# New estimates for three groups of operations in a kernel whose order is planned from estimates

## The chip, the cores and the metric

The kernel runs on one core of a Trainium2 chip. The core has a matrix engine (PE in the profile, with its weight loads as PEld), a vector engine (DVE), a scalar engine (ACT), a general engine (POOL) and a queue that issues the transfers from HBM (SP). Each engine takes its own instructions in the order in which they stand in the program and waits at each for the semaphores of others. The metric is the device time of one launch in microseconds (us), as a median of several runs.

## The reference

Two blocks are computed one after the other on 256 tokens with 1024 features, in float32:

```python
def first_block(x, c, ...):                      # two layers
    mod = einsum('bd,ldm->lbm', silu(c), w_mod) + b_mod
    for i in range(2):
        sh_m, sc_m, g_m, sh_f, sc_f, g_f = split(mod[i], 6)
        h = x * (1 + sc_m) + sh_m
        y = even_mixer(h, ...) if i == 0 else odd_mixer(h, ...)
        x = layer_norm(ALPHA * x + (1 + g_m) * y, ...)
        h = x * (1 + sc_f) + sh_f
        x = layer_norm(ALPHA * x + (1 + g_f) * swiglu(h, ...), ...)
    return x

def hybrid_layer(h, ...):                        # second block, 16 + 256 tokens
    proj = rmsnorm(h) @ w_in                     # nine outputs of 1024
    o = hgrn2_chunked(q, k, v, log(f))           # recurrence over tokens
    merged = sigmoid(gate_a) * rmsnorm(o) * silu(g_out) + sigmoid(gate_b) * b * dwconv(c * x)
    h = h + merged @ w_out
    a, val = split(rmsnorm(h) @ w_up, 2)
    return rmsnorm(h + (silu(dwconv(a)) * val) @ w_down)
```

`even_mixer` holds two attentions (stick-breaking, and one over the 64 best keys of each query), `odd_mixer` the differential attention: two softmaxes per head, one taken from the other with a weight.

## The kernel before, in words

The matrices are read from HBM once, 230 MB in all, and split into two parts that the matrix engine takes in its one-pass float32 form: a slab lands in `stage`, ACT copies it rounded to `whi` (mm3's high part), DVE subtracts that copy from the slab to `wlo`, and every product is made three times (`mm3`: high by high, high by low, low by high). Most of PE's rows are such products with 256 or 258 columns. Six buffers each of `whi` and `wlo`, three of `stage` and three of `mst` bound how far the stream can run ahead.

`mst` is a second stream: the modulation matrix comes in 96 chunks of 512 KB, and DVE makes each into one column of `mod` (`mod_chunks`), one scalar_tensor_tensor per chunk. They are spread over the layers in which they are not yet needed.

Nothing in the program is written in its final order. All operations are recorded by `Plan` in the order of the mathematics, with a due time that is their number plus a bias (`LAG`, `XLAG`, `BIAS`). `Plan.order` (L246 on) then runs a list schedule: each engine takes, whenever it is free in the plan, the operation with the earliest due time of those whose inputs are ready and for which a buffer is free. How long an operation keeps its engine in the plan is what `Plan.cost` (L171 to L207) says. `Plan.issue` sends the operations out in that order, so that all instructions carry its line, L428 (L427 for ACT's table loads). What `cost` says is therefore never on the chip, but the order on each engine is what comes out of it, and so is the buffer that each tile gets.

The places of which the prediction speaks:

- `Norm.add` (L723 on) is called for the eight feature chunks of a residual. DVE makes the residual, ACT its square, DVE and ACT the operand of the next product, and POOL adds residuals and squares to two running sums, `lns1` and `lns2`. When the last chunk is in, PE sums both over the partitions by products with one column (`ps_s`, a constant by `lns1` or `lns2`), and all of the norm follows from these. Rows of the next product group (`norm.U`, 258 columns) can stand ahead of them on PE.
- `gen_diff` (L1225 on) is one head of the differential attention: a score product (`ps_i`) that needs `q` and `kz`, which DVE adds up from a half that POOL has multiplied (`rot`, in `rope_parts`); a softmax on DVE and ACT into `e`; a transpose of `e` on PE.
- `gen_hgrn` (L1446 on), called for two halves of the heads, starts with a chain of 14 small additions on POOL (`su`, L1456). ACT takes their exponential, DVE multiplies it into `kd`, and PE transposes `kd` (L1465).
- `Rms.add` (L1383 on) is the norm of the second block, with one running sum (`racc`) on POOL.

## Time and profile before

| | |
|---|---|
| median of 3 runs | 1172.05 us (1165.66 to 1173.66) |
| span of the profiled execution (first to last instruction) | 1163.9 us |
| PE busy | 1125.9 us, 97% of the span |
| DVE busy | 912.5 us, 78% |
| ACT busy | 726.0 us, 62% |
| POOL busy | 118.2 us, 10% |
| HBM read | 229.81 MB, 198 GB/s over the span |

The profile has one execution, and of that one the span is known and no time of its own beside it. A share of busy time is a mean over stages with different limits; what a change is worth is read from the stage, at the wait that ends last there. Times in the rows below are us from the start of the span, unless ns is said.

### The profile page before, as it was taken

To read this page: it belongs to the slowest core of one execution; us is meant where nothing else is said; L and a number is where in the kernel's file an instruction comes from. 1 tells how busy PE (TensorE), PEld (TensorE's weight loads), DVE (VectorE), ACT (ScalarE), POOL (GpSimd) and SP (SyncE) were. 2 spreads that over 40 slices of the span, in tenths; PEclk is the share of its full clock that TensorE was granted. 3 is DMA by queue.
4 is the path that set the end of the run, shared out by engine and by line. 5 is a ranking of instruction groups with operands and counts; after the bars stand their busy time and mean duration, and the time that the engine had idled before them with its cause. 6 is when DMAs were issued, how large, how long until landed. Compare 5 with 4: busy or idle time off the path is not lost.

```text
span 1163.9 us, 22101 instructions
## 1 busy us (share of the span) xinstructions
PE 1125.9 (97%) x8769; PEld 1077.6 (93%) x8769; DVE 912.5 (78%) x1676; ACT 726.0 (62%) x1316; POOL 118.2 (10%) x127
## 2 busy tenths in 40 slices
PE   5999989999999999999999999999999999999997
PEld 4885889999999779899999999999999999999996
DVE  6799889988999999885558896896659978866642
ACT  3558657545448987664445567786758766655541
POOL 0110220000231302200003402000010011000011
PEclk9999989999999999899999999999999999999999
DMA  9938647998985425365544625244433325555441
GB/s 352 410 131 309 236 163 279 350 328 301 339 327 193 143 104 194 140 246 189 181 171 178 232 88 182 86 169 154 172 110 145 144 100 193 200 188 189 168 163 37
DMA packets 42248, 232.29 MB, mean 200 GB/s; under 512 B 4640, under 2 KB 6176, under 8 KB 24096
## 3 DMA queue, kind: packets, MB, share of 16 engines
q1 hardware_dynamic: 42144, 230.87, 54.4%
q8 instruction: 69, 1.13, 0.4%
q14 instruction: 35, 0.29, 0.1%
HBM read 229.81 MB, written 1.05 MB: 198 GB/s over the span
## 4 chain that ended last, share of the span: by engine, by line
PE 77%; DVE 11%; ACT 4%; DMA 4%; issue 2%; POOL 2%; DVEq 0%; SPq 0%; ACTq 0%; POOLq 0%
PE pa L428 77%; DVE w L428 5%; DVE wlo L428 3%; ACT w L428 2%; DMA mst<-in_wmod_dram 2%; POOL w L428 2%; DVE sm L428 2%; DVE mst L428 1%; ACT whi L428 1%; DMA whi<-in_w_dram 1%; DMA cst<-in_cst_dram 1%; ACT L427 0%; DMA vec<-in_vecs_dram 0%; ACT sm L428 0%; ACT scb L428 0%
## 5 line engine op out<-in xcount | busy, mean ns | idle before, releaser
L428 PE MATMUL pa<-w,whi 128*128 128x256 f32 (+4 forms) x5104 | 919.4, 288 | 8.5 <-DMA whi<-in_w_dram 7.6
L428 PEld LDWEIGHTS pa<-w,whi 128*128 128x128 f32 x5104 | 769.7, 190 | 16.9 <-ACT w L428 6.3
L428 PE MATMUL pa<-w,wlo 128*128 128x256 f32 (+3 forms) x2608 | 661.5, 289 | 0.0
L428 ACT ACTIVATE whi<-stage 128x1024 fp32r<-128x1024 f32 (+1 forms) x330 | 339.5, 1041 | 247.7 <-PE pa L428 217.8
L428 DVE TENSOR_TENSOR wlo<-stage,whi 128x1024 fp32r<-128x1024 f32 (+1 forms) x330 | 404.1, 1234 | 100.3 <-ACT whi L428 94.0
L428 PEld LDWEIGHTS pa<-w,wlo 128*128 128x128 f32 x2608 | 465.5, 190 | 7.0 <-issue 3.9
L428 ACT ACTIVATE w<-w 128x256 fp32r<-128x256 f32 (+9 forms) x257 | 117.3, 470 | 80.6 <-DVE w L428 66.9
L428 POOL TENSOR_TENSOR w<-w,w 128x256 f32<-128x256 f32 (+2 forms) x93 | 84.1, 917 | 521.6 <-ACT w L428 291.2
L428 ACT ACTIVATE w<-pa 128x256 f32<-128x256 f32 (+12 forms) x298 | 108.0, 392 | 46.0 <-PE pa L428 41.7
L428 DVE TENSOR_TENSOR w<-w,w 128x256 fp32r<-128x256 f32 (+7 forms) x263 | 121.5, 480 | 19.2 <-ACT w L428 15.7
L428 DVE SCALAR_TENSOR_TENSOR mst<-mst,scb 128x1024 f32<-128x1024 f32 x90 | 109.3, 1226 | 11.8 <-DMA mst<-in_wmod_dram 11.8
L428 DVE TENSOR_TENSOR w<-w,pa 128x256 f32<-128x256 f32 (+2 forms) x146 | 58.9, 418 | 60.9 <-PE pa L428 51.1
L427 ACT ACT_TABLE_LOAD x63 | 80.8, 1283 | 1.8 <-PEq L1832 0.7
L428 PE MATMUL pa<-w,w 128*128 128x128 f32 (+8 forms) x340 | 71.6, 336 | 1.2 <-DVE w L428 0.9
L428 PEld LDWEIGHTS pa<-w,w 128*128 128x128 f32 (+4 forms) x340 | 42.8, 176 | 10.6 <-issue 2.8
L428 PE MATMUL pa<-cst,w 128*128 128x128 f32 (+4 forms) x218 | 38.8, 268 | 12.6 <-POOL w L428 6.3
L428 PEld LDWEIGHTS pa<-cst,w 128*128 128x128 f32 (+2 forms) x218 | 27.8, 167 | 22.1 <-issue 7.5
L428 POOL TENSOR_TENSOR w<-w 128x256 f32<-128x256 f32 x4 | 3.2, 801 | 392.3 <-DVE w L428 392.3
L428 PE MATMUL pa<-w 128*128 128x128 f32 x240 | 35.0, 275 | 0.2 <-DVE w L428 0.2
L428 PE MATMUL pa<-whi,w 128*128 128x512 f32 x96 | 32.9, 417 | 0.0
L428 PEld LDWEIGHTS pa<-w 128*128 128x128 f32 x240 | 31.4, 191 | 0.4 <-issue 0.4
L428 POOL TENSOR_TENSOR w<-w,sinT 128x512 f32<-128x512 f32 (+1 forms) x14 | 20.4, 1454 | 107.0 <-ACT w L428 82.3
(145 smaller groups left out, 541.3 us busy)
## 6 DMA issues: line engine op xcount, KB each, us to landing
mst<-in_wmod_dram SPq DMA_DIRECT2D x90, 512.0 KB, 5.5
stage<-in_wgu_dram SPq DMA_DIRECT2D x44, 1024.0 KB, 5.0
stage<-in_wi_dram SPq DMA_DIRECT2D x36, 1024.0 KB, 4.8
stage<-in_wup_dram SPq DMA_DIRECT2D x22, 1024.0 KB, 4.8
stage<-in_wd_dram SPq DMA_DIRECT2D x24, 896.0 KB, 4.5
stage<-in_w_dram SPq DMA_DIRECT2D x15, 1024.0 KB, 7.1
stage<-in_wo_dram SPq DMA_DIRECT2D x12, 1024.0 KB, 4.8
stage<-in_wd_dram SPq DMA_DIRECT2D x12, 1024.0 KB, 4.8
```

The lines of the kernel that those rows point to most:

```text
L427: self.nc.scalar.preload_act_table_set(tables[i])
L428: fn(*[real(a) for a in args], **{k: real(a) for k, a in kw.items()})
```

## The change

Only `Plan.cost` is changed. A product in the one-pass form of 256 columns or more is put at 0.452 ns per column rather than 1/2.4 (118.2 rather than 109.2 ns at 256). An operation of ACT or DVE that writes to fewer than 128 partitions gets 90 ns on top. POOL's operations, which had 100 ns and 2.2 ns per element, get formulas of their own: 60 and 0.87 for a memset, 200 and 1.0 for an affine_select, 260 and 2.45 for the rest (an addition of 256 columns: 887 rather than 663 ns, one of 8 columns: 280 rather than 118). No instruction is added or removed on PE, DVE, POOL or SP; the numbers set the order, the buffer of each tile and the places of ACT's table loads.

```diff
             if reads[0].dtype == F32:
                 return max(214.0, 4 * n / 2.4 + 5)
-            return (n if n >= 256 or reads[0].dtype == BF16 else 4 * n) / 2.4 + 2.5
+            if reads[0].dtype == BF16:
+                return n / 2.4 + 2.5
+            return 0.452 * n + 2.5 if n >= 256 else 4 * n / 2.4 + 5
         if eng == "ACT":
...
-            return src + n * 0.833 + 93.0 * ptr + (90.0 if len(writes) > 1 else 0.0)
+            held = 90.0 if writes[0].shape[0] < 128 else 0.0
+            return src + n * 0.833 + 93.0 * ptr + held + (90.0 if len(writes) > 1 else 0.0)
         if eng == "POOL":
-            return 100.0 + n * 2.2
+            if op == "memset":
+                return 60.0 + n * 0.87
+            if op == "affine_select":
+                return 200.0 + n * 1.0
+            return 260.0 + n * 2.45
...
-        return 66.0 + 64.0 * ptr + n * (0.52 if fast else 1.04)
+        held = 90.0 if writes[0].shape[0] < 128 else 0.0
+        return 66.0 + 64.0 * ptr + held + n * (0.52 if fast else 1.04)
```

What the order makes of it is shown at three places. In these rows the number behind a name is that of the tile's buffer and of the write that filled it; L428 of before is L436 of the change.

**The modulation stream.** SP's queue at the end of the first swiglu's down projection and the start of the second layer. Before:

```order
L428 DMA stage_3752<-in_w_dram 128x2048
L428 DMA mst_3789<-in_wmod_dram 128x1024
L428 DMA stage_3811<-in_w_dram 128x2048
L428 DMA mst_3850<-in_wmod_dram 128x1024
L428 DMA stage_3867<-in_w_dram 128x2048
L428 DMA mst_3907<-in_wmod_dram 128x1024
L428 DMA stage_3926<-in_w_dram 128x2048
L428 DMA mst_3969<-in_wmod_dram 128x1024
L428 DMA mst_3990<-in_wmod_dram 128x1024
```

And now, at the same place in the queue:

```order
L436 DMA mst_3512<-in_wmod_dram 128x1024
L436 DMA mst_3556<-in_wmod_dram 128x1024
L436 DMA stage_3566<-in_wd_dram 128x1792
L436 DMA stage_3612<-in_w_dram 128x2048
L436 DMA mst_3627<-in_wmod_dram 128x1024
L436 DMA mst_3640<-in_wmod_dram 128x1024
L436 DMA mst_3674<-in_wmod_dram 128x1024
L436 DMA stage_3694<-in_w_dram 128x2048
L436 DMA mst_3730<-in_wmod_dram 128x1024
```

Up to three chunks now stand between two slabs where there was one or two, and the slabs come later in the queue: ahead of the first slab of the second layer (`stage_3611` before, `stage_3612` now) there are 85 chunks of this stream rather than 77. DVE's own rows of the chunks move along. Before, the last ten of them ran between 349 and 512 us; now all stand ahead of the place that was reached at 349 us.

**The norm of the differential attention's residual.** PE, where the next product group (258 columns) meets the sums of the norm (`cst` by a running sum, 128x1). Before:

```order
L428 MATMUL pa_5488<-w_12_5254,whi_5418 128x258
L428 MATMUL pa_5486<-w_18_5259,whi_5402 128x258
L428 MATMUL pa_5488<-w_18_5259,whi_5418 128x258
L428 MATMUL pa_5486<-w_12_5254,wlo_5451 128x258
L428 MATMUL pa_5495<-w_12_5254,whi_5428 128x258
L428 MATMUL pa_5481<-w_12_5254,whi_5386 128x258
L428 MATMUL pa_5481<-w_18_5259,whi_5386 128x258
L428 MATMUL pa_5495<-w_18_5259,whi_5428 128x258
L428 MATMUL pa_5481<-w_12_5254,wlo_5415 128x258
L428 MATMUL pa_5486<-w_12_5254,whi_5402 128x258
L428 MATMUL pa_5508<-cst_100,w_4_5342 128x1
L428 MATMUL pa_5508<-cst_100,w_4_5431 128x1
```

Now:

```order
L436 MATMUL pa_5483<-w_12_5242,whi_5372 128x258
L436 MATMUL pa_5483<-w_18_5252,whi_5372 128x258
L436 MATMUL pa_5483<-w_12_5242,wlo_5397 128x258
L436 MATMUL pa_5491<-w_12_5242,whi_5400 128x258
L436 MATMUL pa_5493<-cst_100,w_3_5318 128x1
L436 MATMUL pa_5491<-w_18_5252,whi_5400 128x258
L436 MATMUL pa_5497<-w_12_5242,whi_5412 128x258
L436 MATMUL pa_5497<-w_18_5252,whi_5412 128x258
L436 MATMUL pa_5493<-cst_100,w_9_5367 128x1
L436 MATMUL pa_5493<-cst_100,w_3_5318 128x1
```

Fourteen rows of the next group stood ahead of the first sum; now it is four. On DVE, which feeds the sums, the third of four residuals moves behind two weight subtractions (`wlo`) and two operand splits that it stood ahead of.

**The small chain of the first HGRN half.** DVE, where it prepares POOL's chain: the product with 260 columns and the one after it belong to the convolution, the COPY of 4 columns is the chain's first value, and the pair 128x4x16 is `kd`, which waits for the chain. Before:

```order
L428 TENSOR_TENSOR w_7_8428<-w_7_8428,pa_8388 128x260
L428 TENSOR_SCALAR w_4_8443<-w_7_8428,vec_98 128x258
L428 COPY w_10_8450<-w_2_8279 128x4
L428 MEMSET w_10_8450 128x4 x2
L428 TENSOR_TENSOR wlo_8456<-stage_8156,whi_8433 128x1024
L428 TENSOR_TENSOR wlo_8476<-stage_8314,whi_8447 128x1024
L428 MEMSET w_10_8450 128x4
L428 SCALAR_TENSOR_TENSOR w_4_8443<-w_7_8428,vec_98,w_4_8443 128x258 x2
L428 MEMSET w_6_8515 128x256
L428 MEMSET w_3_8521 32x128
L428 TENSOR_TENSOR wlo_8525<-stage_8314,whi_8466 128x1024
L428 TENSOR_TENSOR w_6_8515<-w_10_8450,w_2_8279 128x4x16 x2
```

Now, the first rows and, behind three memsets and two rows of the convolution, the last:

```order
L436 TENSOR_TENSOR wlo_8387<-stage_8212,whi_8371 128x1024
L436 TENSOR_TENSOR wlo_8416<-stage_8289,whi_8400 128x1024
L436 TENSOR_TENSOR wlo_8429<-stage_8289,whi_8411 128x1024
L436 TENSOR_TENSOR wlo_8443<-stage_8326,whi_8424 128x1024
L436 TENSOR_TENSOR w_7_8436<-w_7_8436,pa_8396 128x260
L436 TENSOR_SCALAR w_10_8465<-w_7_8436,vec_98 128x258
L436 COPY w_3_8469<-w_2_8240 128x4
```

```order
L436 TENSOR_TENSOR wlo_8499<-stage_8326,whi_8448 128x1024
L436 TENSOR_TENSOR w_10_8465<-w_10_8465,pa_8450 128x258
L436 TENSOR_TENSOR wlo_8544<-stage_8404,whi_8528 128x1024
L436 TENSOR_TENSOR wlo_8561<-stage_8404,whi_8549 128x1024
L436 TENSOR_TENSOR w_6_8488<-w_3_8469,w_2_8240 128x4x16 x2
```

Four weight subtractions that stood behind the chain's first value now stand ahead of it, and between that value and `kd` there are again three, of later slabs. On ACT, in the same way, four weight copies (`whi`) now stand ahead of the copy that the 260-column product reads. On PE, 21 more rows stand ahead of the transpose of `kd`: 17 products of 258 columns and 4 products of 128 columns in full float32.

## Rows read from the trace of the kernel before

**Rows 1.** The page: span, PE, and groups of instructions with busy time, mean ns, idle.

```profile
span 1163.9 us, 22101 instructions
...
PE 1125.9 (97%) x8769; PEld 1077.6 (93%) x8769; DVE 912.5 (78%) x1676; ACT 726.0 (62%) x1316; POOL 118.2 (10%) x127
...
L428 ACT ACTIVATE whi<-stage 128x1024 fp32r<-128x1024 f32 (+1 forms) x330 | 339.5, 1041 | 247.7 <-PE pa L428 217.8
L428 DVE TENSOR_TENSOR wlo<-stage,whi 128x1024 fp32r<-128x1024 f32 (+1 forms) x330 | 404.1, 1234 | 100.3 <-ACT whi L428 94.0
```

**Rows 2.** PE's waits over the whole span: total us, times, longest.

```profile
PE pa L428 <- DVE w L428: 6.4, 10, 2.1
PE pa L428 <- POOL w L428: 6.3, 4, 3.0
```

**Rows 3.** PE's waits from 349 to 470 us, the differential attention's stage.

```profile
PE pa L428 <- DVE w L428: 3.7, 5, 2.1
```

**Rows 4.** Stretches: us, PE, PEld, DVE, ACT, POOL busy, clock, DMA share, GB/s.

```profile
175.00:349.00 174.00, 174.00 (x1477) 174.00 (x1475) 157.06 (x235) 94.71 (x143) 16.55 (x14) 1.00 0.88 322
...
436.00:465.00 29.00, 28.61 (x228) 27.41 (x227) 28.17 (x72) 22.82 (x61) 6.42 (x6) 1.00 0.56 198
...
716.38:718.60 2.22, 1.74 (x16) 1.55 (x14) 0.10 (x1) 0.00 (x0) 1.59 (x8) 1.00 0.76 236
...
721.37:728.19 6.82, 6.82 (x32) 6.46 (x33) 5.62 (x9) 5.23 (x7) 0.00 (x0) 0.52 0.45 155
```

**Rows 5.** The tile `mst`: DVE's rows (ns min/median/max, first and last), and DVE's wait.

```profile
L428 DVE SCALAR_TENSOR_TENSOR mst<-mst,scb x90: 1202/1220/1755, 5.9 to 512.1; 128x1024 f32<-128x1024 f32 x90
...
  DMA mst<-in_wmod_dram: 11.8, 11
```

**Rows 6.** POOL's groups by shape: busy us, mean ns, idle before.

```profile
L428 POOL TENSOR_TENSOR w<-w,w 128x256 f32<-128x256 f32 x59 | 66.5, 1149 | 242.6 <-ACT w L428 190.7 <-DVE w L428 51.8
...
L428 POOL TENSOR_TENSOR w<-w,w 128x8 f32<-128x8 f32 x28 | 10.0, 358 | 178.3 <-DVE w L428 131.2 <-ACT whi L428 45.1
```

**Rows 7.** Order of time at two norms: start, duration, what, [idle before, releaser].

```profile
465.41 1.25 DVE L428 SCALAR_TENSOR_TENSOR w<-pa,mod,w 128x256 f32<-128x256 f32 x3
...
467.77 1.83 DVE L428 SCALAR_TENSOR_TENSOR w<-w,lnv1lmg,w 128x256 fp32r<-128x256 f32 x2
...
466.02 6.69 POOL L428 TENSOR_TENSOR w<-w,w 128x256 f32<-128x256 f32 x6 [1.96 <-DVE w L428]
...
471.10 1.05 PE L428 MATMUL pa<-cst,w 128*128 128x1 f32 x8 [2.08 <-POOL w L428]
...
153.20 0.38 PE L428 MATMUL pa<-cst,w 128*128 128x1 f32 x2 [2.98 <-POOL w L428]
```

**Rows 8.** Order of time at the first HGRN half, by engine.

```profile
709.91 4.87 ACT L428 ACTIVATE whi<-stage 128x1024 fp32r<-128x1024 f32 x5
...
710.88 0.42 DVE L428 TENSOR_TENSOR w<-w,pa 128x260 f32<-128x260 f32 x1 [3.64 <-PE pa L428]
...
711.95 6.86 POOL L428 TENSOR_TENSOR w<-w,w 128x8 f32<-128x8 f32 x14 [45.06 <-ACT whi L428]
...
717.39 0.38 PE L428 MATMUL pa<-w,w 128*128 128x128 f32 x2
...
717.74 0.38 PE L428 MATMUL pa<-w,w 128*128 128x128 f32 x2
719.59 0.27 PE L428 MATMUL pa<-cst,w 128*32 128x128 f32 x1 [1.48 <-DVE w L428]
```

**Rows 9.** PE in order of time: the second half, the second block's norm, two attention waits.

```profile
856.04 0.27 PE L428 MATMUL pa<-cst,w 128*32 128x128 f32 x1 [0.52 <-DVE w L428]
...
963.50 0.38 PE L428 MATMUL pa<-cst,w 128*128 128x1 f32 x2 [0.68 <-POOL w L428]
...
381.94 0.67 PE L428 MATMUL pa<-w,w 128*128 128x256 f32 x2 [0.89 <-DVE w L428]
...
408.25 0.41 PE L428 MATMUL pa<-cst,w 128*128 128x128 f32 x2 [2.06 <-DVE w L428]
```

## The prediction

> **What bounds the kernel now.** I read the page first. PE is busy for 1125.9 of 1163.9 us [rows 1], and it never gets through its products faster than one every 118 ns: 1477 rows, nearly all of them products of 256 columns, fill the 174.00 us from 175 to 349 without a gap, 174.00 / 1477 = 0.118 us each [rows 4]. So PE's own work is fixed, the change doesn't touch it, and only what PE waits for can move. Second, PE's waits: DVE's results cost it 6.4 us in 10 waits and POOL's 6.3 in 4 [rows 2]. Apart from these there is the start, where the first weights arrive; the order of the first 60 us is the same before and now. Third, the granted clock by stretches: the clock falls to its 1.2 GHz level four times, once at the end of the kernel and three times just behind a long wait of PE; the last of these three, from 721.37 to 728.19, shows 0.52 [rows 4]. In such a stretch PE does half its work, so each costs 6.82 / 2 = 3.4 us. Fourth, the weights: ACT waited 217.8 us for PE to free a buffer before its copies [rows 1], so nearly everywhere the stream of weights is ahead of PE.
>
> All of the gain that an order can bring is therefore 12.7 us of waits and at most three falls of the clock, 10.2 us. The loss has no such bound.
>
> **The change part by part.** Nothing is removed or added. The reader of the diff expects the plan to come closer to the chip. It does so in part: POOL's addition of 256 columns goes from 663 to 887 ns in the plan, but takes 1149 here, and that of 8 columns from 118 to 280, but takes 358 [rows 6]. I go through the places where PE waits, and ask at each who is late now.
>
> *The modulation stream* moves most. Ten chunks more than before lie ahead of 349 us on DVE, at 1.22 us each [rows 5] 12.2 us. From 175 to 349 DVE has 174.00 - 157.06 = 16.9 us to spare [rows 4], so they fit. For SP, eight chunks of 0.52 MB more stand ahead of the second layer's first slab; at the 322 GB/s of this stretch at a share of 0.88 (366 at all of it), 4.2 MB take 11.5 us, and 0.12 of 174 us is 20.9. They fit too, with little left, and the lead of the weights covers the rest. Where the chunks leave there is nothing to win: from 436 to 465, where four of the ten stood, PE is busy for 28.61 of 29 us [rows 4]. I take 0; without the cover it is the second rival.
>
> *The norm after the differential attention.* PE reaches the sums ten rows of 258 columns earlier at the first of them and eight earlier at the pair that reads the second sum, 8 x 0.118 = 0.9 us less work ahead of it. POOL's six additions end at 466.02 + 6.69 = 472.71 [rows 7], and the last pair needs the third residual. Before, three residuals follow each other from 465.41 to 466.66. Now the third comes behind two operand splits (1.83 for two) and two weight subtractions (1.23 each [rows 1]): 465.41 + 0.42 + 1.83 + 2.47 + 0.42 = 470.55. POOL's last pair, 6.69 / 6 = 1.115 us each, then ends at 470.55 + 2.23 = 472.8, 0.1 later than it does. So +1.0, between +0.3 (the first pairs, which can start sooner, free POOL) and +2.
>
> *The norm in the first layer.* PE waits 2.98 us for the same sum until 153.20 [rows 7]; it comes there 3 rows, 0.35 us, sooner, and the third residual is behind one weight subtraction more. POOL's queue of additions hides most of that. +0.5, between 0 and +1.2.
>
> *The first HGRN half.* PE has finished what stands ahead of the transpose at 717.74 + 0.38 = 718.12 and waits 1.48 us, to 719.59 [rows 8]. Now it has 21 rows more: 17 of 0.118, and 4 products in full float32, whose pitch together with one 258-column product is 717.74 - 717.39 = 0.35, so 0.23 each: 2.0 + 0.9 = 2.9 us. It comes at 721.0. By that alone the wait is gone. But who feeds the chain is late too: on ACT four of the five weight copies that begin at 709.91 (4.87 / 5 = 0.97 each) now come first, and DVE's four subtractions behind them, the last of which can start only when the fourth copy is there, at 709.91 + 3.9 = 713.8, and ends at 715.0. The 260-column product then starts 4.1 us later than its 710.88, and the chain at 711.95 + 4.1 = 716.1. If the chain takes its 6.86 us, it ends at 722.9; from the chain's end to the transpose it was 719.59 - 718.81 = 0.78, so `kd` is there at 723.7, and PE waits 2.7 us: +1.2. If the chain is as fast as in its last eight steps, 2.22 / 8 = 0.28 [rows 4], it takes 3.9 us, `kd` is there at 720.8, and the wait is gone: -1.5. Those eight fast steps ran while DVE did next to nothing (0.10 of 2.22 us). Now again three weight subtractions stand between the chain's first value and `kd`, so the slow case is the nearer: chain 6.4, `kd` at 723.2, wait 2.2, +0.7. The fall of the clock at 721.37 then stays.
>
> The Trainium skill, in "SBUF — State Buffer", section "SBUF: two separate sides", says that a POOL operation that reads SBUF and a DVE operation with two inputs in SBUF lock each other out for the whole of an instruction. By that rule no price per size is right for POOL, and the plan's 280 ns per step would be true only where no weight subtraction lies beside the chain; the sum would have -1.5 here where DVE is free and +1.2 where it is not. The row of the eight fast steps agrees with it.
>
> *The second half.* PE has 15 rows more ahead of the transpose, 14 x 0.118 + 0.23 = 1.9 us, and the wait of 0.52 [rows 9] is covered, unless `kd`, now behind one more weight subtraction of 1.23, comes later too. -0.4, between -0.5 and +0.7.
>
> *The norm of the second block.* PE comes 5 rows, 0.6 us, later; the residual that POOL adds last comes behind one more weight subtraction, 1.23. The wait of 0.68 [rows 9] becomes 1.2. +0.5, between -0.6 and +1.
>
> *The differential attention.* DVE's five waits from 349 to 470 us sum to 3.7 [rows 3]. The score product that waits 0.89 at 381.94 stands 37 rows earlier, 4.4 us; its two additions on DVE come ahead of three weight subtractions, 3.7 us, so the wait grows to some 1.6, +0.7. The transpose that waits 2.06 at 408.25 stands 17 rows earlier, but its softmax on ACT loses two weight copies and two scalings that stood ahead of it (3 us) and starts sooner with its scores: I take half of the wait, -1.0. The others change place. -0.3, between -3.7 (all waits gone) and +4 (as much again).
>
> **The sum**: 0 + 1.0 + 0.5 + 0.7 - 0.4 + 0.5 - 0.3 = +2.0 us, against the profiled span of 1163.9: 1165.9. The median of the runs lies 8.1 us above that span, so 1174 us for the median.
>
> **The rivals.**
>
> *The plan is nearer to the chip, and PE's waits shrink* (faster). For it: more rows ahead of both `kd` transposes, and earlier softmaxes. HGRN's first half at -1.5 with its fall of the clock gone (-3.4), the second at -0.5, the attention at -3.7, and the norms at their lower bounds (+0.3, 0, -0.6): -9.4, 1163 us. Against it: the late chain above, which decides: `kd` must be there by 721.0. To be faster by over 1% it must also lose the fall behind the norm at 472, though that norm's wait grows.
>
> *The modulation stream starves the weights* (slower). DVE's wait for chunks that have not landed was 11.8 us in 11 waits [rows 5], and in its queue such a wait holds up every weight subtraction behind it. With 12.2 of its 16.9 us taken, 4.7 are left; from there on the weights fall behind. If the chunks of 175 to 349 wait as long as all did, 11.8 - 4.7 = 7.1 us, and a lead that is used up, PE stops for these, and a fall of the clock of 3.4 follows: 2 + 10.5, 1184 to 1185 us.
>
> *The order hardly matters*: PE waits little, each wait is passed from one row to another, and the sum is within 1 us of 0: 1171 to 1173.
>
> **How the numbers follow.** The forecast's own sum, with its terms between their bounds, gives 1169 to 1180 and has 0.52. The unchanged time has 0.18. The faster rival has 0.12, of which less than half passes 1%. The slower one has 0.18. The likeliest is 1174. To leave out 2 in 10, I drop the better half of the faster rival and the worse part of the slower, whose waits could be longer than I took: 1163 to 1187. About 1% (1160.3 to 1183.8 us) is what a measurement of this kernel can tell from no change. Faster than that: 0.08, the part of the faster rival that also loses a second fall of the clock. Slower: 0.18 and a rest of the forecast in which a new wait brings a fall, 0.20 together. The same: 0.72.
>
> **What would show it.** Right: PE's row count and pitch as now; POOL's sums end near 472.8 with a longer wait of PE, some 3 us, ahead of them; the chain of the first half starts near 716 and PE still waits for `kd`; the fall of the clock near 721 is there; no wait of PE for `wlo` from 175 to 349. Wrong: a wait for `whi` or `wlo` in the first swiglu, DVE idle behind `mst` loads for longer than 11.8 us in all, or a chain at 0.28 us a step.

## The result, and the profile after

The changed kernel takes 1176.45 us (median of 6 runs, 1175.25 to 1179.82), the kernel before 1169.26 us in the same comparison (6 runs, 1165.66 to 1173.66). The ratio is 1.0074, with a 95% interval of 1.0052 to 1.0096: 0.7% slower, within 1%. The profiled execution grew from 1163.9 us [rows 1] to 1173.4.

The page of the changed kernel, its span and busy times; then PE's waits over the whole span (total us, times, longest):

```profile
span 1173.4 us, 22108 instructions
PE 1130.3 (96%) x8769; PEld 1083.2 (92%) x8769; DVE 912.8 (78%) x1676; ACT 724.9 (62%) x1314; POOL 118.3 (10%) x127
```

```profile
PE pa L436 <- POOL w L436: 8.7, 3, 3.6
...
PE pa L436 <- DVE w L436: 7.2, 8, 1.8
```

Against [rows 2], the waits for POOL and DVE have grown from 12.7 to 15.9 us, by 3.2. That is a third of the 9.5 us by which the span grew. PE's busy time grew by 4.4 although its 8769 products are the same: some of them ran at the lower clock. Span and mean granted clock, first of the kernel before, then of the changed one:

```profile
core 0: 1163.9 us, clock 0.989
```

```profile
core 0: 1173.4 us, clock 0.982
```

1163.9 x 0.011 = 12.8 us and 1173.4 x 0.018 = 21.1 us: the granted clock alone took 8.3 us more. (A wait that lies inside a stretch at low clock is counted here too, so this and the waits don't simply add; and a stretch costs somewhat less than half its length, as the last section shows.) The stretches of the changed kernel, in the columns of [rows 4]; all but the first line are falls to the 1.2 GHz level:

```profile
175.00:349.00 174.00, 174.00 (x1476) 174.00 (x1475) 163.85 (x251) 93.16 (x143) 17.80 (x13) 1.00 0.91 335
```

```profile
154.99:165.24 10.25, 9.34 (x42) 9.04 (x43) 8.56 (x16) 4.38 (x7) 2.06 (x2) 0.51 0.75 264
```

```profile
352.97:359.80 6.83, 6.83 (x34) 6.83 (x35) 2.29 (x8) 2.12 (x4) 0.00 (x0) 0.51 0.58 217
479.30:486.10 6.80, 6.79 (x32) 6.79 (x33) 4.32 (x10) 3.17 (x6) 0.83 (x1) 0.51 0.46 157
677.25:680.65 3.40, 3.40 (x18) 3.40 (x17) 1.97 (x15) 0.41 (x2) 0.00 (x0) 0.52 0.55 229
735.30:738.70 3.40, 3.40 (x19) 3.40 (x18) 1.91 (x4) 3.37 (x6) 0.00 (x0) 0.52 0.08 31
868.40:871.80 3.40, 3.40 (x17) 3.28 (x17) 2.22 (x4) 3.13 (x5) 0.00 (x0) 0.52 0.72 287
```

The kernel before has three such stretches of 6.8 us ahead of its end; the one of [rows 4] at 721 is gone, and there are now six.

**Where the time went.** I compared the time of PE's n-th product in both traces, counted in order, and read off how the distance changes. Predicted and measured, in us:

| place | predicted | measured |
|---|---|---|
| top-k mask, 80 to 100 us | not in the sum | +1.8 |
| norm in the first layer, 155 | +0.5 | +3.3, then -0.8 |
| first FFN, 175 to 349 | 0 | 0.0 |
| end of the first FFN, 352 | 0 (the modulation stream) | +5.2 |
| differential attention | -0.3 | -1.5 |
| norm behind it, 479 | +1.0 | +0.9 |
| start of the second block, 677 | not in the sum | +1.9 |
| first HGRN half | +0.7 | -4.9, then +1.7 |
| second HGRN half | -0.4 | +0.3 |
| norm of the second block | +0.5 | +0.8 |

These rows make +8.7 of the 9.3 us that lie between the two traces at 1140 us; the rest is small, +0.5 of it from 100 to 140 us. Both columns of time are single executions. What the table shows at 677 us and in the second HGRN half holds a half-clock stretch each, and such stretches come and go there between executions of the same order (last section), so those two rows can't be put down to the change.

The largest loss. DVE in order of time, at the end of the first FFN in the changed kernel (start, duration, what):

```profile
348.08 1.77 DVE L436 TENSOR_TENSOR wlo<-stage,whi 128x1024 fp32r<-128x1024 f32 x1
349.77 1.21 DVE L436 SCALAR_TENSOR_TENSOR mst<-mst,scb 128x1024 f32<-128x1024 f32 x1
...
351.13 1.22 DVE L436 TENSOR_TENSOR wlo<-stage,whi 128x1024 fp32r<-128x1024 f32 x1
352.28 0.48 DVE L436 SCALAR_TENSOR_TENSOR w<-pa,mod,w 128x256 f32<-128x256 f32 x1
```

The last row is the eighth residual of the FFN's norm. It comes behind a modulation chunk, its sum into `mod` (0.17 us, not shown) and a weight subtraction. In the kernel before it ended 0.5 us ahead of PE's products, which had no wait (DVE, then PE):

```profile
345.86 0.48 DVE L428 SCALAR_TENSOR_TENSOR w<-pa,mod,w 128x256 f32<-128x256 f32 x1
...
346.83 1.62 PE L428 MATMUL pa<-cst,w 128*128 128x1 f32 x14
```

In the changed kernel PE waits for it, as the third of these rows shows; the others are the norms, to be read beside [rows 7, 9]:

```profile
155.42 0.59 PE L436 MATMUL pa<-cst,w 128*128 128x1 f32 x2 [3.63 <-POOL w L436]
157.78 1.01 PE L436 MATMUL pa<-cst,w 128*128 128x1 f32 x4 [0.48 <-DVE w L436]
...
352.81 2.90 PE L436 MATMUL pa<-cst,w 128*128 128x1 f32 x14 [1.83 <-DVE w L436]
...
479.31 0.53 PE L436 MATMUL pa<-cst,w 128*128 128x1 f32 x2 [3.53 <-POOL w L436]
...
973.40 0.38 PE L436 MATMUL pa<-cst,w 128*128 128x1 f32 x2 [1.50 <-POOL w L436]
```

1.83 us of wait and 6.83 / 2 = 3.4 of half clock right behind it make the 5.2.

### The profile page after: what moved, and what is told of

Its sections match the earlier page's. It is cut to its first block, busy times and chain, and to the rows that moved or that the text cites. A ratio compares the mean times of both kernels' runs of the same rounds, so it can differ in the third digit from the quotient of the medians.

```text
span 1173.4 us, 22108 instructions
## 1 busy us (share of the span) xinstructions
PE 1130.3 (96%) x8769; PEld 1083.2 (92%) x8769; DVE 912.8 (78%) x1676; ACT 724.9 (62%) x1314; POOL 118.3 (10%) x127
## 4 chain that ended last, share of the span: by engine, by line
PE 79%; DVE 10%; ACT 5%; DMA 3%; issue 2%; POOL 1%; DVEq 0%; SPq 0%; POOLq 0%; ACTq 0%
PE pa L436 79%; DVE w L436 4%; ACT w L436 4%; DVE wlo L436 3%; DMA mst<-in_wmod_dram 2%; DVE mst L436 2%; DVE sm L436 1%; ACT whi L436 1%; DMA cst<-in_cst_dram 1%; POOL w L436 1%; DMA vec<-in_vecs_dram 0%; ACT sm L436 0%; ACT scb L436 0%; DVEq L1846 0%; SPq L436 0%
## 5 line engine op out<-in xcount | busy, mean ns | idle before, releaser
L436 PE MATMUL pa<-w,whi 128*128 128x256 f32 (+4 forms) x5104 | 922.8, 289 | 9.6 <-DMA whi<-in_w_dram 7.5
L436 PEld LDWEIGHTS pa<-w,whi 128*128 128x128 f32 x5104 | 771.4, 191 | 17.6 <-ACT w L436 6.0
L436 PE MATMUL pa<-w,wlo 128*128 128x256 f32 (+3 forms) x2608 | 662.2, 290 | 0.1
L436 ACT ACTIVATE whi<-stage 128x1024 fp32r<-128x1024 f32 (+1 forms) x330 | 341.0, 1041 | 256.2 <-PE pa L436 230.4
L436 DVE TENSOR_TENSOR wlo<-stage,whi 128x1024 fp32r<-128x1024 f32 (+1 forms) x330 | 404.3, 1232 | 104.0 <-ACT whi L436 99.2
L436 PEld LDWEIGHTS pa<-w,wlo 128*128 128x128 f32 x2608 | 466.3, 191 | 9.0 <-issue 5.2
L436 ACT ACTIVATE w<-w 128x256 fp32r<-128x256 f32 (+9 forms) x257 | 117.2, 469 | 82.2 <-DVE w L436 78.5
L436 POOL TENSOR_TENSOR w<-w,w 128x256 f32<-128x256 f32 (+2 forms) x93 | 85.8, 936 | 521.8 <-ACT w L436 291.3
L436 ACT ACTIVATE w<-pa 128x256 f32<-128x256 f32 (+11 forms) x298 | 108.4, 391 | 43.4 <-PE pa L436 37.5
L436 DVE TENSOR_TENSOR w<-w,w 128x256 fp32r<-128x256 f32 (+7 forms) x263 | 120.1, 474 | 9.4 <-ACT w L436 6.5
L436 DVE SCALAR_TENSOR_TENSOR mst<-mst,scb 128x1024 f32<-128x1024 f32 x90 | 109.8, 1231 | 14.5 <-DMA mst<-in_wmod_dram 14.2
L436 DVE TENSOR_TENSOR w<-w,pa 128x256 f32<-128x256 f32 (+2 forms) x146 | 59.0, 417 | 61.3 <-PE pa L436 54.3
L436 PE MATMUL pa<-w,w 128*128 128x128 f32 (+8 forms) x340 | 67.9, 330 | 0.4 <-ACT w L436 0.2
L436 PE MATMUL pa<-cst,w 128*128 128x128 f32 (+4 forms) x218 | 41.9, 282 | 15.6 <-POOL w L436 8.7
L436 PEld LDWEIGHTS pa<-cst,w 128*128 128x128 f32 (+2 forms) x218 | 30.8, 185 | 24.9 <-POOL w L436 9.6
L436 PEld LDWEIGHTS pa<-w,w 128*128 128x128 f32 (+4 forms) x340 | 41.7, 171 | 8.9 <-issue 3.9
L436 POOL TENSOR_TENSOR w<-w 128x256 f32<-128x256 f32 x4 | 3.8, 949 | 397.9 <-DVE w L436 397.9
L436 PE MATMUL pa<-w 128*128 128x128 f32 x240 | 37.4, 274 | 0.0
L436 PE MATMUL pa<-whi,w 128*128 128x512 f32 x96 | 33.5, 420 | 0.0
L436 PEld LDWEIGHTS pa<-w 128*128 128x128 f32 x240 | 32.8, 190 | 0.0
L436 POOL TENSOR_TENSOR w<-w,sinT 128x512 f32<-128x512 f32 (+1 forms) x14 | 17.4, 1242 | 108.6 <-ACT w L436 103.8
```

The costliest lines, as they stand in the source:

```text
L436: fn(*[real(a) for a in args], **{k: real(a) for k, a in kw.items()})
```

## The experiments

Two kinds of edit were made. Prices are changed in `Plan.cost`. Pieces of the order are moved by a list that `issue` applies to the plan's order before anything is sent out; the numbers are those that `record` gives the operations, and each piece is named in words:

```diff
         order, slot, tables = self.order()
+        for ids, where, anchor in MOVES:
+            order = [i for i in order if i not in ids]
+            at = order.index(anchor) + (where == "after")
+            order[at:at] = ids
```

All ratios are to the kernel before, timed in turn with it on the same chip; kernels of different comparisons are therefore compared by their ratios. "Clock" is the mean over the runs of span x (1 - granted clock), "rest" what remains of the span. The kernel before shows 15.6 to 17.2 and 1149.0 to 1150.0 in the four comparisons; the changed kernel 22.7 and 1152.4.

| kernel | median us | ratio (95%) | clock | rest |
|---|---|---|---|---|
| changed kernel | 1176.45 | 1.0074 (1.0052 to 1.0096) | 22.7 | 1152.4 |
| part_product | 1186.47 | 1.0176 (1.0153 to 1.0199) | 27.5 | 1158.4 |
| part_gpsimd | 1166.10 | 0.9996 (0.9985 to 1.0008) | 15.0 | 1149.7 |
| part_partitions | 1173.37 | 1.0049 (1.0027 to 1.0070) | 17.8 | 1153.8 |
| without_product | 1168.22 | 0.9999 (0.9981 to 1.0016) | 14.7 | 1151.3 |
| vector_prices_up | 1172.77 | 1.0042 (1.0020 to 1.0065) | 16.9 | 1154.1 |
| back_four | 1168.53 | 1.0003 (0.9990 to 1.0016) | 15.2 | 1151.3 |
| chunk_behind | 1172.78 | 1.0057 (1.0036 to 1.0078) | 22.3 | 1149.4 |
| chunk_ahead | 1173.83 | 1.0051 (1.0027 to 1.0074) | 21.6 | 1150.4 |
| hgrn_rows | 1165.21 | 0.9981 (0.9962 to 1.0000) | 14.4 | 1149.4 |
| sums_first | 1166.58 | 0.9982 (0.9963 to 1.0001) | 15.8 | 1148.3 |
| sums_first_2 | 1164.83 | 0.9987 (0.9972 to 1.0002) | 15.4 | 1148.0 |
| before_mended | 1164.38 | 0.9968 (0.9952 to 0.9984) | 14.7 | 1148.2 |

### Which price

**part_product**, the product's price alone in the kernel before:

```diff
-            return (n if n >= 256 or reads[0].dtype == BF16 else 4 * n) / 2.4 + 2.5
+            if reads[0].dtype == BF16:
+                return n / 2.4 + 2.5
+            return 0.452 * n + 2.5 if n >= 256 else 4 * n / 2.4 + 5
```

> Kernel before with one of the new prices alone: the one-pass product of 256 columns at 118.2 ns instead of 109.2 ns in the plan. In the order it gives, VectorE has the same modulation chunks ahead of the last residual of the first layer's first-half FFN as the changed kernel (96 of them, 86 in the kernel before), the same two splits ahead of the third residual of the second layer's first norm, and TensorE has as many rows ahead of the first HGRN half's decay transposes as the kernel before (4913; before 4916, changed kernel 4937). Theory A (the product price carries the loss, the GpSimd price the gain): a wait of about 1.8 us for VectorE near 352 us followed by a half-clock stretch of 6.8 us, so +5 us there, +1 us at the second layer's first norm, and the fall of the clock at 721 us stays: about 1175 us, 6 us above the kernel before. Rival B (the wait near 352 us needs the whole change, because GpSimd's later rows set it): no such wait, 1169 to 1171 us.

(The edit takes along the diff's constant for narrower products, 5 ns for 2.5; without_product below puts both back.) 1.8% slower: worse than theory A, and worse than the whole change. PE's waits:

```profile
PE pa L430 <- DVE w L430: 15.3, 13, 3.7
PE pa L430 <- POOL w L430: 10.6, 4, 4.6
```

The wait near 352 us came as expected (1.53 us, then a half-clock stretch of 6.8), and so did waits that I had not expected: 2.9 us at 127 us, and more in the differential attention, where PE waits 8.1 us for DVE from 349 to 470, that one included, against 3.7 [rows 3]. Rival B is out: that wait needs no GpSimd price.

**part_gpsimd** and **part_partitions**, the other two prices alone:

```diff
-            return 100.0 + n * 2.2
+            if op == "memset":
+                return 60.0 + n * 0.87
+            if op == "affine_select":
+                return 200.0 + n * 1.0
+            return 260.0 + n * 2.45
```

> Kernel before with the GpSimd prices alone. In the order it gives, the first FFN's last residual has the same 86 chunks ahead of it as in the kernel before, and TensorE has 30 more rows ahead of the first HGRN half's decay transposes (4946 against 4916). Theory A: the wait for the decays of 1.5 us and the half-clock stretch of 6.8 us behind it go (-4.9 us), nothing is added near 352 us, other places move by under 1 us each: about 1164 us, 5 us below the kernel before. Rival B (the rows ahead of the transposes do not matter; the wait goes in the changed kernel because everything there starts later by chance of the clock): the wait and the half-clock stretch near 721 us stay, 1168 to 1171 us.

```diff
+        held = 90.0 if writes[0].shape[0] < 128 else 0.0
-        return 66.0 + 64.0 * ptr + n * (0.52 if fast else 1.04)
+        return 66.0 + 64.0 * ptr + held + n * (0.52 if fast else 1.04)
```

(the same `held` in ACT's line)

> Kernel before with the 90 ns for writes to under 128 partitions alone. In the order it gives, the first FFN's last residual has 87 chunks ahead of it (86 before), the first layer's norm has two splits of weights ahead of its third residual as in the changed kernel (one in the kernel before), and the decay transposes of the first HGRN half stand 3 rows later than before. Theory A: the longer wait at the first layer's norm comes with it (+1 us, and +2.5 us if the half-clock stretch there grows from 6.8 to 10.2 us), the rest as before: 1170 to 1172 us. Rival B (this price too brings the wait near 352 us): 1174 us or more.

The GpSimd prices alone change nothing that can be measured (0.9996). In their trace the wait at the first HGRN half is down from 1.48 to 0.68 us and the half-clock stretch at 721 is gone, 4.4 us in all, but 3.4 come back within 20 us, 1.3 of them by a wait for ACT and 1.7 by a half-clock stretch of 3.4: theory A had the place right and the balance wrong. The part-partition price costs 0.5%, more than theory A gave it, though neither its first FFN's end nor its decays are worse: about 4 us of its loss come in the differential attention, where PE now also waits for a weight subtraction (1.47 us at 386 us) and of which I had said nothing. At the first norm the stretch did grow to 10.2 us, but the wait shrank to 2.3, so that only 0.7 us are lost there.

**without_product**, the changed kernel with that one price taken back:

```diff
-            return 0.452 * n + 2.5 if n >= 256 else 4 * n / 2.4 + 5
+            return (n if n >= 256 else 4 * n) / 2.4 + 2.5
```

> Changed kernel with one of its prices taken back: the one-pass product of 256 columns at 109.2 ns in the plan again; the GpSimd prices and the 90 ns for part-partition writes stay. In the order it gives, 86 chunks stand ahead of the first FFN's last residual (kernel before 86, changed kernel 96), one split of weights instead of two ahead of the third residual of the second layer's first norm, and TensorE has 19 more rows ahead of the first HGRN half's decay transposes than in the kernel before. Theory A (the product's price, beside the others too, is what fills VectorE's queue ahead of the sums): no wait and no half-clock stretch at 353 us, no wait for the decays at 721 us: 1166 to 1169 us, 8 to 10 us under the changed kernel. Rival B (the parts add, the price for part-partition writes brings its 6 us with it): 1172 to 1174 us.

0.9999: theory A, and the parts don't add (the two prices that are left had 0.9996 and 1.0049). PE and clock at the end of the first FFN:

```profile
349.00:357.00 8.00, 8.00 (x70) 8.00 (x69) 7.29 (x18) 4.04 (x9) 0.00 (x0) 1.00 0.95 336
```

No gap and no fall. So the loss needs the product's price, and that price is right: PE made 1476 products in 174.00 us here, 0.118 each. In the plan, 9 ns more for each make 1476 x 0.009 = 13.3 us in which DVE has room, and ten chunks take 12.2 us. That the plan filled just this room is an estimate and not shown: in the next run all DVE prices go up by the same factor, and only three of the ten chunks leave.

**vector_prices_up**, the rival to that: is a PE that is too fast in the plan a margin for DVE, which a higher price for DVE would give as well?

```diff
-        return 66.0 + 64.0 * ptr + held + n * (0.52 if fast else 1.04)
+        return 1.082 * (66.0 + 64.0 * ptr + held + n * (0.52 if fast else 1.04))
```

> Changed kernel with all VectorE prices in the plan 8.2% higher, the same factor by which the change raised the one-pass product. In the order it gives, 93 chunks (changed kernel 96, before 86) and one split stand ahead of the first FFN's last residual, no split between the second and third residual of the first layer's norm, and 26 more rows ahead of the decay transposes than in the kernel before. Theory A (what counts is the rows that stand ahead of a sum): the chunk and the split still stand there, so the wait of 1.8 us and the half-clock stretch near 353 us stay; the first norm gets 1 to 2 us shorter: 1172 to 1176 us. Rival B (the low product price had worked as a margin on VectorE, so that the ratio of the two prices decides): with the ratio put back, the time goes back too: 1165 to 1169 us.

1172.8 us, in theory A's range. The chunk and the split still stand ahead of the residual, and PE still waits:

```profile
349.15 1.72 PE L436 MATMUL pa<-cst,w 128*128 128x1 f32 x14 [1.43 <-DVE w L436]
```

The ratio of the two prices alone does not decide, so rival B is out. Theory A is borne out in part: the wait is there, but the half-clock stretch behind it is 3.4 us and not 6.8. This profile ends 7.1 us above that of the kernel before: 3.2 come at this place and 6.5 between 660 and 708 us, by a half-clock stretch of 6.8 us at 669 and by copies of ACT that PE waits for, and other places give some of it back.

### Which rows

**back_four**, four pieces of DVE's order in the changed kernel put back:

```diff
+MOVES = [
+    ([1011, 1014, 1192], 'after', 981),
+    ([1016, 1197], 'after', 987),
+    ([4811, 4812, 3075], 'after', 3037),
+    ([4349, 4389, 4570, 4355, 4392], 'after', 4359),
+    ([212, 298], 'after', 352),
+]
```

> Changed kernel with four pieces of VectorE's order put back as in the kernel before, and no row of another engine but the transfers that refill the weight buffers they free: the copy of one modulation chunk behind the bias copies of the top-k mask (about 75 us); two splits of weights and one behind the third and fourth residual of the first layer's norm (about 150 us); one chunk, its modulation sum and one split behind the last residual of the first FFN (352 us); the third residual of the second layer's norm ahead of two splits (478 us). Theory A (each lost stretch is caused by the rows that were moved in front of a sum for which TensorE waits): the four places give back 1.4, 2.5, 5.2 and 1 us, with the gain at the first HGRN half kept: 1166 to 1168 us, 2 us under the kernel before. Rival B (the rows only pass their time on: the chunks are done a little later, TensorE waits for a later sum or for weights, and the half-clock stretches come elsewhere): 1173 to 1177 us.

The time of the kernel before (1.0003), so theory A on the whole, 0.5 us above its range. Place by place it does not hold everywhere. The first FFN's end gave back 3.6 of 5.2 us and has no half-clock stretch any more. The norm behind the attention gave back nothing; DVE and PE there:

```profile
471.44 2.88 DVE L447 TENSOR_TENSOR wlo<-stage,whi 128x1024 fp32r<-128x1024 f32 x2
474.24 0.47 DVE L447 SCALAR_TENSOR_TENSOR w<-pa,mod,w 128x256 f32<-128x256 f32 x1
```

```profile
471.28 0.38 PE L447 MATMUL pa<-cst,w 128*128 128x1 f32 x2 [0.70 <-POOL w L447]
474.77 1.39 PE L447 MATMUL pa<-cst,w 128*128 128x1 f32 x6 [2.63 <-DVE w L447]
```

The third residual is early again, but the two subtractions now stand ahead of the fourth: 0.70 + 2.63 in place of 3.53. Here the rows passed their time on, as rival B says.

**chunk_behind** and **chunk_ahead**, one piece by itself, in both directions: in the changed kernel the chunk and its sum behind the residual, in the kernel before one chunk and one weight subtraction ahead of it.

```diff
+MOVES = [
+    ([4811, 4812], 'after', 3037),
+]
```

> Changed kernel with one piece of VectorE's order moved: at the end of the first FFN the last modulation chunk (1.21 us) and its modulation sum go from ahead of the last residual to right behind it; the split that stands there too stays. Theory A (the chunk makes the wait and the wait lets the clock fall): the wait of 1.8 us shrinks to about 0.5 us and the half-clock stretch of 6.8 us at 353 us goes, -1.3 and -3.4 us: 4 to 5 us under the changed kernel. Rival B (the half-clock stretch comes by itself at this place): the wait shrinks, the stretch stays: 1.3 us under the changed kernel. Rival C (the time passes on to the statistics): the wait moves to the transposes behind the sum, nothing is won.

```diff
+MOVES = [
+    ([4097, 3075], 'before', 3037),
+]
```

> Kernel before with the opposite edit: one modulation chunk and one split of weights, 2.3 us of VectorE, moved from behind the last residual of the first FFN to right ahead of it, as the changed kernel has it. In the kernel before that residual ends 0.5 us ahead of its use. Theory A: a wait of 1.8 us near 347 us and a half-clock stretch of 6.8 us behind it that the kernel before does not have: 4 to 5 us above the kernel before. Rival B (VectorE catches up, since it has more idle time there than in the changed kernel): under 1 us. Rival C (the wait comes but the clock stays up): 1.8 us above.

PE's wait and the stretch behind it, first in chunk_behind:

```profile
351.76 1.72 PE L443 MATMUL pa<-cst,w 128*128 128x1 f32 x14 [0.30 <-DVE w L443]
```

```profile
353.64:357.06 3.42, 3.42 (x19) 3.42 (x18) 1.82 (x8) 1.49 (x2) 0.00 (x0) 0.52 0.65 228
```

and in chunk_ahead, with DVE's rows:

```profile
347.27 1.21 DVE L435 SCALAR_TENSOR_TENSOR mst<-mst,scb 128x1024 f32<-128x1024 f32 x1
...
348.42 1.21 DVE L435 TENSOR_TENSOR wlo<-stage,whi 128x1024 fp32r<-128x1024 f32 x1
349.56 0.47 DVE L435 SCALAR_TENSOR_TENSOR w<-pa,mod,w 128x256 f32<-128x256 f32 x1
```

```profile
350.08 1.99 PE L435 MATMUL pa<-cst,w 128*128 128x1 f32 x14 [1.52 <-DVE w L435]
```

```profile
351.24:354.65 3.41, 3.41 (x17) 3.41 (x18) 2.43 (x9) 1.49 (x2) 0.00 (x0) 0.52 1.00 376
```

The wait goes with the chunk, and comes with the chunk and the subtraction. The half-clock stretch does so in part: 6.83 becomes 3.42 in the one (3.1 us won in all at that place), and none becomes 3.41 in the other (3.3 us lost). Over the whole kernel the first is not told apart from the changed kernel: 1.0057 against 1.0074, 2 us, with intervals that overlap, short of theory A's 4 to 5, and its clock is as poor (22.3 against 22.7). The second is 0.51% above the kernel before, 6 us. So two rows of 2.3 us make two thirds of the whole loss in a kernel that has nothing else of the change. Of these 6 us, 3.3 are seen at the place. Over the runs nearly all 6 are granted clock (21.6 against 15.6 us, the rest 1150.4 against 1150.0), and in the profile stretches of 3.4, 6.8 and 6.8 us at 82, 672 and 867 us come on top, where its rows are those of the kernel before. Whether the two rows bring these about is not shown.

**hgrn_rows**, the gain: in the kernel before, the 21 products of the change ahead of the decay transposes, and the one DVE row that two of them need.

```diff
+MOVES = [
+    ([7064], 'before', 6989),
+    ([7062, 7096, 7063, 7072, 7097, 7073, 7074, 7098, 7075, 7099, 7112,
+      7100, 7113, 7101, 7114, 7115, 7102, 7116, 7103, 7117, 7104], 'before', 6991),
+]
```

> Kernel before with one piece of the changed kernel's order: the 21 products that the change puts ahead of the decay transposes in the first HGRN half (17 weight products of 258 columns, 4 of 128) and the one VectorE row on which two of them rest; all else stays. Theory A (those rows are the work TensorE does while it waited, and the wait was what let the clock fall): the wait of 1.5 us and the half-clock stretch of 6.8 us at 721 us go and nothing is given back: 5 us under the kernel before. Rival B (the clock falls a little later, behind the 24 one-column products that follow the transposes, whatever stands ahead of them): the wait goes, a half-clock stretch of 3.4 us or 6.8 us comes within 15 us of it: 1.5 to 3 us under the kernel before. Rival C (the decays are needed there because of another wait): no change at all.

Rival B, at that place: -4.9 us for the wait and the stretch of [rows 4, 8], and +2.0 right behind it across a shorter one, as in the changed kernel (-4.9, +1.7). In all 0.9981, with an interval that ends at 1.0000. Two stretches of this run:

```profile
664.34:671.17 6.83, 6.83 (x33) 6.83 (x33) 3.28 (x17) 0.41 (x2) 0.88 (x1) 0.51 0.43 156
...
725.78:729.20 3.42, 3.42 (x19) 3.42 (x18) 3.06 (x5) 3.39 (x5) 0.00 (x0) 0.52 0.46 194
```

and the first of them in the kernel before:

```profile
664.34:671.17 6.83, 6.83 (x56) 6.69 (x57) 4.97 (x20) 1.62 (x5) 1.59 (x1) 1.00 0.66 257
```

Up to 710 us the two kernels have the same rows in the same order on every engine. The stretch at 664 is therefore not the work of an order: it came in one execution and not in the other. (Among the 35 runs of the kernel before in this comparison the mean granted clock goes from 0.979 to 0.989.)

The 2 us that come back would do so without the shorter stretch at 726. before_mended, further below, has the same rows here and its clock stays up, and there PE waits for DVE instead:

```profile
731.62 0.46 PE L441 MATMUL pa<-w 128*128 128x128 f32 x2 [1.57 <-DVE w L441]
```

From 708 to 745 us both gain the same on the kernel before, 2.8 us. What the 21 rows give here is bounded by DVE's next result, with the fall of the clock or without.

**sums_first**, **sums_first_2** and **before_mended** use this to look for a faster order. The first has nothing that can wait ahead of a sum at the two norms and the first FFN's end of the changed kernel; the second mends the late weights that this made and puts two more pieces back; the third does the same at the norms of the kernel before and adds the 21 rows. The moves of the first, without those of refilling transfers:

```diff
+MOVES = [
+    ([872], 'after', 981),
+    ([977, 983, 1011, 1014, 1016], 'after', 987),
+    ([1019, 1191], 'after', 1005),
+    ([3075, 3258], 'after', 3055),
+    ([4811, 4812], 'after', 3258),
+    ([4349, 4389], 'after', 4359),
+    ([4355, 4392, 4394], 'after', 4365),
+]
```

> Changed kernel with VectorE's order changed by hand at three places, so that nothing that can wait stands ahead of a sum or of its statistics: in the first layer's norm (148 us) the split ahead of the first two residuals goes behind the third and three splits and two residual parts behind the fourth; at the end of the first FFN (350 us) two splits, one chunk and its modulation sum go behind the last residual and the statistics; in the second layer's norm (473 us) one split stays ahead of the fourth residual and two go behind it. Theory A (only what stands ahead of the last residual counts): against the changed kernel the first FFN's end gives back 5.2 us, the first norm 1 to 2.5 us, the second norm 2 us of wait and 3.4 us more if the clock then does not fall: 1163 to 1167 us, under the kernel before. Rival B (GpSimd's additions, 1.15 us each, set the end of both norms whatever VectorE does): only the first FFN's 5 us come back: 1170 to 1172 us. Rival C (the splits are then late for the products): new waits for weights, 1172 us or more.

Theory A: about 10 us under the changed kernel. At the norm behind the attention the second wait of back_four is gone, and the fall of the clock is there still:

```profile
469.81 0.38 PE L455 MATMUL pa<-cst,w 128*128 128x1 f32 x2 [0.69 <-POOL w L455]
```

```profile
470.00:478.00 8.00, 8.00 (x45) 8.00 (x44) 6.79 (x14) 2.89 (x5) 0.62 (x1) 0.59 0.79 275
```

Rival C held on a small scale: two refilled weights were 0.9 and 1.5 us late.

The second, against the first, again without refilling transfers:

```diff
-    ([977, 983, 1011, 1014, 1016], 'after', 987),
+    ([1011, 1014, 977, 983, 1016], 'after', 987),
-    ([3075, 3258], 'after', 3055),
-    ([4811, 4812], 'after', 3258),
+    ([3075, 3258], 'after', 3037),
+    ([4811, 4812], 'after', 3055),
+    ([212, 298], 'after', 352),
+    ([754, 755, 756], 'before', 766),
```

> The kernel of the run sums_first with the faults its trace showed mended: at the end of the first FFN both splits right behind the last residual and only the chunk behind the statistics (a refilled weight came 1.5 us late); in the first layer's norm the three splits ahead of two residual parts (weights 0.6 and 0.9 us late); and two more pieces put as in the kernel before: one chunk behind the bias copies of the top-k mask (1.2 us at 80 us) and the first three products of a bank in the first output projection behind the nine of the other banks (1.5 us at 124 us). Theory A (the rows ahead of sums are the whole loss, and it adds up place by place): 3 to 5 us under sums_first in the sum of its waits, 1160 to 1164 us, under the kernel before by 3 to 6 us. Rival B (places that do not touch the clock give back only their waits, and the half-clock stretches come anyway at one place or another): 1164 to 1167 us.

1.7 us under sums_first between the medians, but against the kernel before the two can't be told apart (0.9987 and 0.9982); rival B. In its profile a half-clock stretch of 6.8 us stands at 961 us, where that of sums_first has none.

The third, on the kernel before:

```diff
+MOVES = [
...
+    ([872], 'after', 981),
+    ([1011, 977, 1014, 983], 'after', 987),
+    ([4349], 'before', 4389),
+    ([4355], 'after', 4365),
+]
```

(the line left out stands for the two moves of hgrn_rows; a refilling transfer that moves along is left out too)

> Kernel before with the gains of the earlier runs and none of the changed kernel's losses: the 21 products and the one VectorE row of the run hgrn_rows ahead of the decay transposes, and VectorE's order at the two norms as in sums_first_2 (in the first layer the first two residuals ahead of a split and the fourth ahead of two splits and two residual parts; in the second layer the fourth residual ahead of one residual part). Theory A (waits that are taken away ahead of a half-clock stretch count twice): 1.5 us less wait at the first norm, 1 us at the second, and 3 us at the HGRN half: 5 to 6 us under the kernel before, 0.995 of its time. Rival B (half-clock stretches come at some place of the program whatever is mended): 1 to 3 us under, 0.998 of its time, and its trace shows as much half-clock time as that of the kernel before.

0.9968: 3 us under the kernel before and 12 under the changed one, the only version whose interval lies below 1. That is between the two theories, and nearer to B: the stretch at 721 is gone from its profile, and others of the same length stand 55 us ahead, as in hgrn_rows, and at 858, four in all ahead of its end where the kernel before has three. At the first norm PE waits as long as before, 2.02 us for the sum and then 0.99 for a refilled weight against 2.98. The two stretches of time, the second at full clock:

```profile
666.50:673.30 6.80, 6.80 (x32) 6.80 (x33) 2.60 (x16) 0.41 (x3) 0.00 (x0) 0.51 0.39 146
721.37:728.19 6.82, 6.68 (x64) 6.08 (x63) 5.65 (x9) 5.75 (x8) 0.00 (x0) 1.00 0.61 237
```

## Why the prediction was right, and where it was not

**The number.** 1174.0 was forecast, 1176.45 came, inside the range of 1163 to 1187 and on the side that had 0.72. But the sum itself was short: +2.0 against 1176.45 - 1169.26 = 7.2 (6.1 to 11.2 by the interval). The forecast came near because it was set on the median of three runs, 2.8 us above that of six; that is luck.

**The modulation stream, 0: this step failed.** I asked whether the chunks fit in between 175 and 349 us and whether the weights starve. Both answers were right: DVE was busy for 163.85 of 174.00 us, and PE was busy for all of it, without a wait for `wlo`. What I did not ask is what stands at the end of the stretch. A queue that is filled to the brim runs late for its last row, and that row was a residual that PE waits for. The chunk ahead of it costs 1.2 us; without it the wait is 0.30 (chunk_behind). The sign I named for the rival was a poor one: DVE's wait for chunks went from the 11.8 us of [rows 5] to 14.2, and no wait of PE for a weight in that stretch came of it. The tile's rows in the changed kernel:

```profile
L436 DVE SCALAR_TENSOR_TENSOR mst<-mst,scb x90: 1202/1219/1768, 6.0 to 349.8; 128x1024 f32<-128x1024 f32 x90
...
  DMA mst<-in_wmod_dram: 14.2, 13
```

The last chunk starts at 349.8 instead of 512.1: the stream ends right at the sum that it delays.

**The norm behind the attention, +1.0: right in size**, +0.9, by the step given. The third residual (477.07) comes behind both subtractions, and POOL's last pair behind it, here in the changed kernel:

```profile
473.37 1.76 DVE L436 TENSOR_TENSOR wlo<-stage,whi 128x1024 fp32r<-128x1024 f32 x1
...
475.93 1.21 DVE L436 TENSOR_TENSOR wlo<-stage,whi 128x1024 fp32r<-128x1024 f32 x1
477.07 0.47 DVE L436 SCALAR_TENSOR_TENSOR w<-pa,mod,w 128x256 f32<-128x256 f32 x1
477.46 1.21 DVE L436 TENSOR_TENSOR wlo<-stage,whi 128x1024 fp32r<-128x1024 f32 x1
```

```profile
477.68 2.45 POOL L436 TENSOR_TENSOR w<-w,w 128x256 f32<-128x256 f32 x2 [1.96 <-DVE w L436]
```

It was incomplete: back_four shows that the fourth residual sets the same end as soon as the third no longer does.

**The norm in the first layer, +0.5: too small.** The wait of 2.98 [rows 7] became 3.63 + 0.48, +1.1, just inside the bound; the rest of the net +2.5 is its half-clock stretch, 10.25 us instead of 6.8. That half is not the change's for certain. With the rows of the kernel before at that place, the stretch was 6.83 us in two profiles (the kernel before, chunk_ahead) and 3.41 in a third (hgrn_rows); with those of the change it was 10.2 in both profiles that have them (the changed kernel, chunk_behind).

**The first HGRN half, +0.7: wrong.** It gave back 3.2. PE came to the transpose when I said it would (721.0; 731.91 - 11.0 = 720.9). The chain did not start 4.1 us later. In the changed kernel, by engine:

```profile
717.49 1.99 ACT L436 ACTIVATE whi<-stage 128x1024 fp32r<-128x1024 f32 x2
719.98 1.06 ACT L436 ACTIVATE whi<-stage 128x1024 fp32r<-128x1024 f32 x1 [0.49 <-PE pa L436]
```

```profile
722.21 0.42 DVE L436 TENSOR_TENSOR w<-w,pa 128x260 f32<-128x260 f32 x1
```

```profile
723.27 5.18 POOL L436 TENSOR_TENSOR w<-w,w 128x8 f32<-128x8 f32 x14 [47.77 <-DVE w L436]
```

```profile
731.91 0.27 PE L436 MATMUL pa<-cst,w 128*32 128x128 f32 x1
```

PE's rows here stand 11.0 us later than in the kernel before, so the 709.91 at which I had the four copies begin is 720.9 here: by then three were done or under way. I had taken their start from an order in which they came behind other work. The same row of [rows 8] also shows DVE idle for 3.64 us ahead of the 260-column product, waiting for PE; most of the subtractions fit into that time. The 260-column product is late by 722.21 - 11.0 - 710.88 = 0.3 us, the chain takes 5.18 us, and PE finds `kd` ready. The fall of the clock at 721 went with the wait, and a shorter one came 3 us behind the transposes.

**The second half** (+0.3 for -0.4) lies within its bounds: the wait of 0.52 [rows 9] is gone, but a stretch of 3.4 us at half clock follows at 868. With the rows of the kernel before there, that place had none in one profile, 3.4 us in another (hgrn_rows) and 6.8 in a third (chunk_ahead), so the change need not have brought it. **The second block's norm**: +0.8 for +0.5; its wait went from 0.68 [rows 9] to 1.50, by the step given. **The attention**: -1.5 for -0.3, within -3.7 and +4. **Not in the sum**: the wait for the top-k mask at 80 us, where a chunk stands ahead of the mask's copy, +1.8.

**The rivals.** The weights did not starve. The truer plan made no faster order: with the GpSimd prices alone it gained and lost in equal parts, and with the right price of a product it lost most. **The unknown that was not priced** is the clock: I counted its falls as things that a wait removes or adds, left the falls that were there in place, and took a fall at half its length, 3.4 us of 6.8, where 3.0 to 3.2 were measured at the start of the second block (last section). Of the 9 us, some 6 are granted clock (22.7 against 15.6 to 17.2), but single falls can't be put down to single rows: chunk_behind has the smaller rest of the two (1149.4; back_four 1151.3), yet 7 us more clock.

**Open.** Which of the three other pieces in back_four, or all of them, bring the clock back is not settled; nor is why the product's price does more harm alone than with the other two. A rival was not tested: of the six orders that new prices gave (the change, its three parts, without_product, vector_prices_up) four were slower, two the same and none faster, so the order before may be a fortunate one that any change of prices spoils. No price of the product other than 109.2 and 118.2 ns was tried.

## What to carry over

Here a list scheduler with a truer price for the engine that bounds the kernel put more rows on another engine, up to the very row that the bounding engine waits for next. So ask of each stretch that gets fuller which row stands at its end, not only whether the sum fits. When rows in front of a sum are moved, move them behind the last input of the sum, since the next input inherits the wait. And price a new wait on PE with the half-clock stretch that may follow it, as a range that starts at nothing: at the end of the first FFN it doubled or tripled the wait, behind the HGRN transposes it hid one, and the wait of 3.31 us at 81 us in the changed kernel has none behind it.

## What the runs showed of the hardware

**The granted clock falls without a wait, and not in each execution.** In the changed kernel the stretch at 677 us follows 26 products of one column in 4 us (14 in 1.62 us at 672.95, 12 in 1.50 at 675.56) and no wait above 0.3 us. The same products came with 6.8 us at half clock in hgrn_rows, chunk_ahead and before_mended and with none in the kernel before, though these four have the same order there. Across such a stretch PE's products came 3.0, 3.2 and 3.0 us later than in the kernel before (hgrn_rows, chunk_ahead, before_mended), less than half of 6.8: in the same 6.83 us PE made 33 rows at half clock in hgrn_rows and 56 at full clock in the kernel before (664.34). Apart from the end, the stretches of all profiles were 3.4, 6.8 or 10.2 us long.

**A weight subtraction on DVE takes up to 1.77 us beside POOL's additions and 1.22 without.** In the changed kernel the one at 473.37 took 1.76 with POOL adding from 471.44 to 475.72, the one at 351.13 took 1.22 with POOL idle, and the one at 477.46, which began just ahead of POOL's pair (477.68), took 1.21. The Trainium skill, in "SBUF — State Buffer", section "SBUF: two separate sides", says that such operations lock each other out, and that the one that starts first has the ports for the whole instruction; these rows agree, and no price in the plan knows of it.
